# Up products of two feed-forward layers as seven block products in place of eight, and down products in five groups

## The chip, the cores and the metric

The kernel runs on one core of a Trainium2 chip. The metric is the device time of one execution in microseconds (us). TensorE (PE) does the matrix products, VectorE (DVE) and ScalarE (ACT) the elementwise work, GpSimd (POOL) some of it too, and SyncE (SP) issues most of the loads.

## The reference

Two layers act on 640 token columns (128 of a prompt, 512 of a sample) of width 1024. The first layer's mixer is a gated delta rule, the second's a neighbourhood attention. After each comes the part that the change touches:

```python
def conv_ffn(h, w_up, conv_w, conv_b, w_down):
    u = dwconv_centred(h @ w_up, conv_w) + conv_b
    val, gate = jnp.split(u, 2, axis=-1)
    return (jax.nn.silu(gate) * val) @ w_down
...
xs = xs + g2s * conv_ffn(rmsnorm(xs, norm2_g[l]) * (1.0 + sc2s) + sh2s,
                         ffn_w_up[l], ffn_conv_w[l], ffn_conv_b[l], ffn_w_down[l])
```

`w_up` is 1024 x 5632 (22 value tiles and 22 gate tiles of 128), `w_down` 2816 x 1024, and the convolution has three taps along the tokens, within the prompt and within the sample apart. Everything is float32.

## The kernel before

Activations lie with their features on the partitions and the 640 columns along the free side. A float32 product is made of three matmuls on a rounded part and a residue: every weight tile `w` is cast by ScalarE to `wh` (L376) and VectorE forms `wl = w - wh` (L378); h is kept as `hh` and `hl`, eight tiles of 128 features each. `pass3` then adds `wh*hh`, `wh*hl` and `wl*hh` in PSUM (L388, L389, L390), in two column halves of 384 and 256 (`HALVES_U`, `HALVES_R`).

`ffn` (one call per layer) goes over 22 pairs, value tile i (`uv`) and gate tile i (`ug`). For a pair `dense` loads each tile (512 KB), splits it and makes 8 x 2 x 3 matmuls into a PSUM tile `duv` or `dug`. Then `conv` scales with the middle tap on ScalarE (L440) and adds the outer taps on VectorE (L445; four instructions a tile, 511 and 127 columns), ScalarE takes silu of the gate, VectorE multiplies (L560), and the product is split again into `F` (L562, L563). After the groups of tiles 0 to 7 and 8 to 14, `into_residual` multiplies the group's F with the down weights (`wdn`) and adds the result to the residual X with `residual` (L454); the last group, 15 to 21, goes through `into_residual_split`, which does one column half after the other so that the next normalization (`hl` L348, `nt` L343) can start on the first.

The order on each engine is set by a scheduler from the written order, priorities and the pools' buffers; `chain` holds TensorE to the written order of products in the first layer. Weights pass through a ring of two tiles each of `wst`, `wh` and `wl`. `between` interleaves modulation sums (`ada_rows`: VectorE instructions of 512 columns, L252, on weights `adr` that the GpSimd queue loads) and, in the first layer, the preparation of attention bias tables. The first pair of a layer is made while the second half of h is still being normalized (`hooks`).

Of the kernel before, what the change touches and what calls it, by code (L numbers as in the profile page):

```python
# [57 lines left out]
GROUPS = ((0, 8), (8, 15), (15, 22))  # L58
# [29 lines left out]
class Net:  # L88
    def __init__(self, ctx, tc, a):
# [5 lines left out]
        self.wide = False  # L95
        self.hooks, self.strict = [], False
# [313 lines left out]
    def dense(self, src, name, base=UBASE, halves=HALVES_U):  # L410
        w = self.weights(src, KT, name)
        ps = self.pd.tile([128, 1024], F32, tag="d", name=f"d{name}")
        for cols in halves:
            self.prod(ps, base, w, KT, self.hmov, cols)
        return ps
# [4 lines left out]
    def dense_many(self, srcs, names, norm):  # L420
# [11 lines left out]
        return [ps for _, ps in out]  # L432

# [24 lines left out]

    def into_residual(self, srcs, kt, movs, l, gi, name, first={}, between=None):
        late = []  # L460
        for m in range(KT):
            w = first.get(m) or self.weights(srcs[m], kt, f"{name}{m}")
            ps = self.pd.tile([128, 1024], F32, tag="d", name=f"r{name}{m}")
            if m < 2:
                late.append((w, ps))
                for half in (0, 1):
                    self.prod(ps, RBASE, w, kt, movs, HALVES_R[half], ks=range(kt - 1))
                if m < 1:
                    continue
            else:  # L470
                late = [(w, ps)]
            for i, (w, ps) in enumerate(late, m + 1 - len(late)):
                for half in (0, 1):
                    self.prod(ps, RBASE, w, kt, movs, HALVES_R[half], ks=range(kt - 1, kt) if m < 2 else None)
                for half in (0, 1):
                    self.residual(ps, i, half, l, gi)
            if between and m > 1:
                between(None)

    def half_bank(self, name, i, half):  # L480
        if self.wide and i % 2 == 1:
            return self.pa.tile([128, 512], F32, tag="g", name=name)
        return self.pd.tile([128, 1024 if self.wide else 512], F32, tag="d", name=name)
# [41 lines left out]
    def ffn(self, l, fp, norm, norms, between=None):  # L525
# [3 lines left out]
        fcb = self.smv("fcb").rearrange("p (l t) -> p l t", l=2)[:, l]  # L529
        def hold(name, n):  # L530
            if name[-1] == "5":
                return fp.tile([128, 2 * W], F32R, tag="F", name=name, bufs=9)[:, 16 : 16 + n]
            size = KT if name[-1] in "01" else NFT - GROUPS[-1][0]
            return fp.tile([128, size * 128], F32R, tag=name[:2] + name[-1], name=name, bufs=1)[:, :n]

        for grp, (g0, g1) in enumerate(GROUPS):
            fs = []
            srcs = [a["w_dn"][l, m][:, g0 * 128 : g1 * 128] for m in range(KT)]
            first = {}
            for i in range(g0, g1):  # L540
                if i >= g1 - 2:
                    m = i - g1 + 2
                    first[m] = self.weights(srcs[m], g1 - g0, f"dn{l}{grp}{m}", None, hold)
                up, names = [a["w_up"][l, i], a["w_up"][l, NFT + i]], [f"uv{l}{i}", f"ug{l}{i}"]
                if i == 0:
                    with self.behind(self.marks):
                        pv, pg = self.dense_many(up, names, norm)
                else:
                    pv = self.dense(up[0], names[0])
                    if between:  # L550
                        between(None)
                    pg = self.dense(up[1], names[1])
                with self.tc.high_priority(FHP if i == g1 - 1 else 0):
                    yv = fp.tile([128, W], F32, tag="yv", name=f"yv{l}{i}", bufs=2)
                    yg = fp.tile([128, W], F32, tag="yg", name=f"yg{l}{i}", bufs=2)
                    self.conv(yv, pv, fcw[:, i], fcb[:, i : i + 1])
                    self.conv(yg, pg, fcw[:, NFT + i], fcb[:, NFT + i : NFT + i + 1])
                    c = slice(0, W)
                    nc.scalar.activation(yg[:, c], yg[:, c], AF.Silu)
                    nc.vector.tensor_tensor(yv[:, c], yv[:, c], yg[:, c], ALU.mult)  # L560
                    f = fp.tile([128, 2 * W], F32R, tag="F", name=f"F{l}{i}", bufs=9).rearrange("p (a w) -> p a w", a=2)
                    nc.scalar.copy(f[:, 0, c], yv[:, c])  # L562
                    nc.vector.tensor_tensor(f[:, 1, c], yv[:, c], f[:, 0, c].bitcast(F32), ALU.subtract)  # L563
                fs.append(f)
                if between:
                    between(i)
            movs = lambda k, fs=fs: (fs[k][:, 0, :], fs[k][:, 1, :])
            if g1 < NFT:
                self.into_residual(srcs, g1 - g0, movs, l, 5, f"dn{l}{grp}", first, between)
            else:  # L570
# [1094 lines left out]
```

## Time and profile before

| | |
|---|---|
| median of 3 runs | 1871.53 us (1865.12 to 1872.86) |
| the profiled execution | 1872.86 us, span 1871.1 us, granted TensorE clock 0.98 |
| first up product of the first layer, last of the second | 583.3 us, 1804.3 us |
| up products | 4224 matmuls (half of 384, half of 256 columns) |
| down products | 2112 matmuls, the same shapes |
| instructions of POOL in the whole span | 498 |

How to read the rows: in the table by stretches, `us, PE busy (x) PEld busy (x) DVE busy (x) ACT busy (x) POOL busy (x), PEclk, DMA share, GB/s` stand behind the window. In groups of instructions the columns are line, engine, operation, written tile <- read tiles, shapes and count | busy us, mean ns of one | idle time before them and its releasers. In the timeline they are start in us, duration in us, engine, line, operation, tiles, shape and count; in brackets the idle time before and who ended it.

### The profile page before, as it was taken

What the parts mean: (1) busy time and instruction counts of PE and PEld (TensorE: products, weight loads), DVE (VectorE), ACT (ScalarE), POOL (GpSimd) and SP (SyncE); (2) the same over time, 40 slices, a digit from 0 to 9 for tenths busy, and PEclk for the clock granted to TensorE, in tenths of its full rate; (3) what the DMA queues carried; (4) which work ended last, traced back from release to release, by engine and by line L of the source; (5) the groups of instructions that cost most, each with busy time, mean ns of one, the idle gap of its engine ahead of it and who ended that gap; (6) DMA issues with size and microseconds to landing.
All of it is one profiled execution on the core that took longest, in us unless ns stands there. A gap on an engine that the chain in (4) does not pass through costs nothing.

```text
span 1871.1 us, 34463 instructions
## 1 busy us (share of the span) xinstructions
PE 1790.4 (96%) x13587; PEld 1702.7 (91%) x13587; DVE 1257.4 (67%) x3093; ACT 725.9 (39%) x1461; POOL 290.3 (16%) x498
## 2 busy tenths in 40 slices
PE   6889999799999999999999999999999999999998
PEld 5878988598899999999999988888899999999998
DVE  6797867487678999754465799555689643543664
ACT  4553445264444341241243444444454322332343
POOL 0245103417003112100000212111141000000000
PEclk9898999799999999999999999999999999999999
DMA  7133233232242455441222344222334312222231
GB/s 299 61 85 108 54 124 108 76 96 61 64 158 86 155 182 163 132 163 54 87 90 80 124 152 139 75 78 65 96 107 136 102 48 78 88 62 77 89 92 57
DMA packets 102482, 194.17 MB, mean 104 GB/s; under 512 B 39496, under 2 KB 59034, under 8 KB 99560
## 3 DMA queue, kind: packets, MB, share of 16 engines
q1 hardware_dynamic: 93376, 161.57, 27.5%
q0 software_dynamic: 8400, 29.87, 5.2%
q8 instruction: 107, 1.75, 0.4%
q14 instruction: 55, 0.45, 0.1%
q10 hardware_dynamic: 544, 0.52, 0.1%
HBM read 183.09 MB, written 12.46 MB: 105 GB/s over the span
## 4 chain that ended last, share of the span: by engine, by line
PE 50%; DVE 4%; issue 2%; DMA 1%; ACT 1%; POOL 0%; DVEq 0%; POOLq 0%; ACTq 0%
PE duv L388 4%; PE duv L390 4%; PE duv L389 4%; PE dug L388 4%; PE dug L389 4%; PE dug L390 4%; PE rdn L388 4%; PE rdn L389 4%; PE rdn L390 4%; PE dqn L388 1%; PE dvn L388 1%; PE no L1346 1%; PE s L1289 1%; PE dvn L390 1%; PE dvn L389 1%
## 5 line engine op out<-in xcount | busy, mean ns | idle before, releaser
L388 PE MATMUL duv<-hh,whuv 128*128 128x256 f32 (+1 forms) x704 | 217.2, 309 | 5.9 <-DVE yv L445 4.0
L388 PE MATMUL rdn<-F,whdn 128*128 128x384 f32 (+1 forms) x704 | 216.1, 307 | 3.3 <-DVE X L454 3.3
L390 PE MATMUL duv<-hh,wluv 128*128 128x256 f32 (+1 forms) x704 | 216.7, 308 | 0.3 <-DVE wluv L378 0.3
L389 PE MATMUL duv<-hl,whuv 128*128 128x256 f32 (+1 forms) x704 | 216.5, 308 | 0.0
L389 PE MATMUL dug<-hl,whug 128*128 128x256 f32 (+1 forms) x704 | 215.9, 307 | 0.0
L390 PE MATMUL dug<-hh,wlug 128*128 128x256 f32 (+1 forms) x704 | 215.9, 307 | 0.0
L388 PE MATMUL dug<-hh,whug 128*128 128x256 f32 (+1 forms) x704 | 215.9, 307 | 0.0
L389 PE MATMUL rdn<-F,whdn 128*128 128x384 f32 (+1 forms) x704 | 215.5, 306 | 0.0
L390 PE MATMUL rdn<-F,wldn 128*128 128x384 f32 (+1 forms) x704 | 215.5, 306 | 0.0
L388 PEld LDWEIGHTS duv<-hh,whuv 128*128 128x128 f32 x704 | 132.8, 189 | 6.4 <-ACT yg L440 4.6
L388 PEld LDWEIGHTS rdn<-F,whdn 128*128 128x128 f32 x704 | 132.4, 188 | 4.0 <-issue 2.1
L454 DVE SCALAR_TENSOR_TENSOR X<-rdn,mods,X 128x128 f32<-128x128 f32 (+1 forms) x144 | 54.9, 434 | 117.6 <-PE rdn L390 117.4
L390 PEld LDWEIGHTS duv<-hh,wluv 128*128 128x128 f32 x704 | 132.9, 189 | 0.6 <-DVE wluv L378 0.6
L389 PEld LDWEIGHTS duv<-hl,whuv 128*128 128x128 f32 x704 | 132.7, 189 | 0.0
L388 PEld LDWEIGHTS dug<-hh,whug 128*128 128x128 f32 x704 | 132.4, 188 | 0.0
L390 PEld LDWEIGHTS dug<-hh,wlug 128*128 128x128 f32 x704 | 132.3, 188 | 0.0
L389 PEld LDWEIGHTS rdn<-F,whdn 128*128 128x128 f32 x704 | 132.2, 188 | 0.0
L390 PEld LDWEIGHTS rdn<-F,wldn 128*128 128x128 f32 x704 | 132.2, 188 | 0.0
L389 PEld LDWEIGHTS dug<-hl,whug 128*128 128x128 f32 x704 | 132.1, 188 | 0.0
L376 ACT CAST whdn<-wstdn 128x896 fp32r<-128x896 f32 (+1 forms) x48 | 47.0, 979 | 209.1 <-PE rdn L389 120.9
L376 ACT CAST whug<-wstug 128x1024 fp32r<-128x1024 f32 x44 | 46.2, 1050 | 142.9 <-PE dug L389 119.4
L378 DVE TENSOR_TENSOR wldn<-wstdn,whdn 128x896 fp32r<-128x896 f32 (+1 forms) x48 | 54.4, 1133 | 56.7 <-ACT whdn L376 56.7
(710 smaller groups left out, 4803.3 us busy)
## 6 DMA issues: line engine op xcount, KB each, us to landing
wstuv<-w_up SPq DMA_DIRECT2D x44, 512.0 KB, 3.5
wstug<-w_up SPq DMA_DIRECT2D x44, 512.0 KB, 3.6
adat<-w_ada SPq DMA_DIRECT2D x20, 1024.0 KB, 5.0
adr<-w_adar POOLq DMA_DIRECT2D x80, 256.0 KB, 3.2
wstdn<-w_dn SPq DMA_DIRECT2D x32, 448.0 KB, 3.4
wstdn<-w_dn SPq DMA_DIRECT2D x16, 512.0 KB, 3.6
adr<-w_adar SPq DMA_DIRECT2D x32, 256.0 KB, 2.9
wstqT<-w_gin SPq DMA_DIRECT2D x8, 512.0 KB, 4.4
```

The lines of the kernel that those rows point to most:

```text
L376: nc.scalar.copy(wh[:, c], st[:, c])
L378: ins = eng.tensor_tensor(wl[:, c], st[:, c], wh[:, c].bitcast(F32), ALU.subtract).ins
L388: nc.tensor.matmul(out, a, mh, start=first, stop=False)
L389: nc.tensor.matmul(out, a, ml, start=False, stop=False)
L390: ins = nc.tensor.matmul(out, b, mh, start=False, stop=last).ins
L454: nc.vector.scalar_tensor_tensor(x, ps[:, base + c0 : base + c1], self.mod(l, gi, m, v), x, ALU.mult, ALU.add)
L1289: nc.tensor.matmul(ss[e][:, o], qb[H[e]], kk[H[e]], start=True, stop=True, tile_position=(64 * e, 0))
L1346: nc.tensor.matmul(O[H[e], cb * 128 : cb * 128 + 128], v_, p_, start=(j == 0), stop=(j == 2), tile_position=(0, 64 * e),)
```

## The change

A pair's value and gate tiles, on the two halves of the 1024 features, form a 2 x 2 block matrix; h, on feature halves and column halves of 320, forms another. The product of 2 x 2 blocks is made with seven block products and sums of blocks (Winograd's form) rather than eight. Of each layer's 22 pairs the first two (`DIRECT`) stay ordinary products; while they run, `blocks` forms the sums of the moving side (`T0`, `T1`, `T2`, and, in place of the right half of the first four feature tiles, a fourth block). For the other 20 pairs `pair` forms sums of weight blocks on GpSimd (`s1`, `s2`, `g0`; L621, L624, L625, L628), casts seven quarters of 512 columns (L551, L552), makes seven products of 12 matmuls with 320 columns and combines them: ScalarE copies two to SBUF (`p1`, `p5`), VectorE makes five adds that read PSUM (L630, L633, L635, L637, L640), GpSimd adds two (L631, L638). The convolution then reads `cv` and `cg` in SBUF, not PSUM. Of the first layer's seven residues, those of products 1 and 3 are formed by GpSimd (`POOLED`).

The downs go in groups of tiles 0-3, 4-7, 8-11, 12-15 and 16-21; a group's downs follow the ups of the pair after it. Eight of the layer-1 modulation vectors' tiles (m = 2) are summed during the attention and not in the first feed-forward layer; the interleaving of the other sums changes. TensorE is held to the written order in the second layer too.

```diff
-GROUPS = ((0, 8), (8, 15), (15, 22))
+GROUPS = ((0, 4), (4, 8), (8, 12), (12, 16), (16, 22))
+NH = W // 2
+DIRECT = 2
+POOLED = ((1, 3), ())
...
+    def quarter(self, src, name, lo=None):
...
+        nc.scalar.copy(wh, src)
+        (lo or nc.vector).tensor_tensor(wl, src, wh.bitcast(F32), ALU.subtract)
...
+    def blocks(self):
+        nc, TT = self.nc, self.nc.vector.tensor_tensor
+        lo, hi = slice(0, NH), slice(NH, W)
+        for k in range(4):
+            b = self.B[k]
+            for i in range(2):
+                nc.gpsimd.tensor_tensor(
+                    b[:, i], self.hh[:, k + 4 * i].bitcast(F32), self.hl[:, k + 4 * i].bitcast(F32), ALU.add
+                )
+            b11, b12, b21, b22 = b[:, 0, lo], b[:, 0, hi], b[:, 1, lo], b[:, 1, hi]
+            TT(b11, b12, b11, ALU.subtract)
+            TT(b12, b22, b12, ALU.subtract)
+            TT(b22, b22, b11, ALU.subtract)
+            TT(b21, b21, b22, ALU.subtract)
+            for t, x in zip(self.T, (b11, b22, b12)):
+                nc.scalar.copy(t[:, k, 0], x)
+                TT(t[:, k, 1], x, t[:, k, 0].bitcast(F32), ALU.subtract)
...
+    def pair(self, l, i, fp, pf):
...
+        P, V = nc.gpsimd.tensor_tensor, nc.vector.tensor_tensor
...
+        P(s1, g0, g1, ALU.add)
+        x = product(5, s1, self.tmov(0), L)
+        nc.scalar.copy(p5, x)
+        P(s2, s1, v0, ALU.subtract)
+        P(g0, v0, g0, ALU.subtract)
+        x = product(1, v0, first, L)
+        nc.scalar.copy(p1, x)
+        P(s1, v1, s2, ALU.subtract)
+        x = product(6, s2, self.tmov(1), L)
+        V(cg1, x, p1, ALU.add)
+        P(cv1, cg1, p5, ALU.add)
+        x = product(3, s1, last, R)
+        V(cv1, x, cv1, ALU.add)
+        x = product(2, v1, last, L)
+        V(cv0, x, p1, ALU.add)
+        x = product(7, g0, self.tmov(2), L)
+        V(cg0, x, cg1, ALU.add)
+        P(cg1, cg0, p5, ALU.add)
+        x = product(4, g1, first, R)
+        V(cg0, x, cg0, ALU.add)
...
-        sums = net.ada_rows([(1, m, t) for m in (3, 4) for t in range(KT)], self.ap_, 2, self.nc.sync)
+        sums = net.ada_rows([(1, m, t) for m in (2, 3, 4) for t in range(KT)], self.ap_, 2, self.nc.sync)
```

The order of instructions shows the change in three places. In these rows the names are written tile <- read tiles with the buffer's number. First VectorE in the second layer, where two pairs follow one another with no downs between. Before (`wluv`, `wlug` residues, L445 taps):

```order
L378 TENSOR_TENSOR wluv_18946<-wstuv_18943,whuv_18945 128x1024
L445 SCALAR_TENSOR_TENSOR yv_18926<-duv_18822,sm,yv_18926 128x127
L445 SCALAR_TENSOR_TENSOR yv_18926<-duv_18822,sm,yv_18926 128x511
L445 SCALAR_TENSOR_TENSOR yv_18926<-duv_18822,sm,yv_18926 128x127
L445 SCALAR_TENSOR_TENSOR yv_18926<-duv_18822,sm,yv_18926 128x511
L378 TENSOR_TENSOR wlug_19001<-wstug_18998,whug_19000 128x1024
L445 SCALAR_TENSOR_TENSOR yg_18927<-dug_18877,sm,yg_18927 128x127
L445 SCALAR_TENSOR_TENSOR yg_18927<-dug_18877,sm,yg_18927 128x511
L445 SCALAR_TENSOR_TENSOR yg_18927<-dug_18877,sm,yg_18927 128x127
L445 SCALAR_TENSOR_TENSOR yg_18927<-dug_18877,sm,yg_18927 128x511
L560 TENSOR_TENSOR yv_18926<-yv_18926,yg_18927 128x640
L563 TENSOR_TENSOR F_18940<-yv_18926,F_18940 128x640
```

Now, of the 23 rows of such an interval, those in its middle (`wlp` are residues of quarters, `pp` the products in PSUM, `s_19043` the next pair's sum from GpSimd):

```order
L552 TENSOR_TENSOR wlp_18954<-s_18892,whp_18953 128x512
L552 TENSOR_TENSOR wlp_18954<-wsv_18890,whp_18953 128x512
L694 TENSOR_TENSOR yv_18871<-yv_18871,yg_18872 128x640
L630 TENSOR_TENSOR cg_18897<-pp_18938,p_18894 128x320
L552 TENSOR_TENSOR wlp_18988<-wsg_18888,whp_18987 128x512
L697 TENSOR_TENSOR F_18885<-yv_18871,F_18885 128x640
L633 TENSOR_TENSOR cv_18896<-pp_18957,cv_18896 128x320
L552 TENSOR_TENSOR wlp_18988<-wsg_18888,whp_18987 128x512
L635 TENSOR_TENSOR cv_18896<-pp_18973,p_18894 128x320
L552 TENSOR_TENSOR wlp_19051<-s_19043,whp_19050 128x512
L552 TENSOR_TENSOR wlp_19051<-wsv_19041,whp_19050 128x512
L637 TENSOR_TENSOR cg_18897<-pp_18991,cg_18897 128x320
```

Adds from PSUM now stand between the residues, and the residue of product 4 (the second `wlp_18988`) stands behind the add L633.

Second, GpSimd in the second layer. Before, the loads of `adr` end its work until the last normalization:

```order
L234 DMA adr_16648<-w_adar 128x512
L234 DMA adr_16654<-w_adar 128x512
L308 TENSOR_TENSOR nstf_19875<-nstf_19875,mhalf 128x3
L308 TENSOR_TENSOR nstf_20095<-nstf_20095,mhalf 128x2
L1661 UNCONDITIONAL_BRANCH
```

Now six instructions stand there for each of 20 pairs (of one pair's interval, between two L638):

```order
L638 TENSOR_TENSOR cg_18593<-cg_18593,p_18591 128x320
L621 TENSOR_TENSOR s_18892<-wsg_18888 128x512
L624 TENSOR_TENSOR s_18893<-s_18892,wsv_18890 128x512
L625 TENSOR_TENSOR wsg_18888<-wsv_18890,wsg_18888 128x512
L631 TENSOR_TENSOR cv_18743<-cg_18744,p_18742 128x320
L628 TENSOR_TENSOR s_18892<-wsv_18890,s_18893 128x512
L638 TENSOR_TENSOR cg_18744<-cg_18744,p_18742 128x320
```

The add L631, for which VectorE's L633 waits, stands behind the three sums of the next pair.

Third, VectorE at the end of the second layer's two direct pairs (`B` are the moving side's blocks, `duv_16754` the second pair's product, `s_16917` the first sum of pair 2). Before there is no such work: taps and residues follow as in the first fence. Now:

```order
L592 TENSOR_TENSOR hl<-B_16521,hh 128x320
L459 SCALAR_TENSOR_TENSOR yv_16868<-duv_16754,sm,yv_16868 128x256
L459 SCALAR_TENSOR_TENSOR yv_16868<-duv_16754,sm,yv_16868 128x127
L459 SCALAR_TENSOR_TENSOR yv_16868<-duv_16754,sm,yv_16868 128x255
L459 SCALAR_TENSOR_TENSOR yv_16868<-duv_16755,sm,yv_16868 128x255
L459 SCALAR_TENSOR_TENSOR yg_16869<-dug_16762,sm,yg_16869 128x127
L459 SCALAR_TENSOR_TENSOR yv_16868<-duv_16755,sm,yv_16868 128x256
L459 SCALAR_TENSOR_TENSOR yg_16869<-dug_16762,sm,yg_16869 128x256
L459 SCALAR_TENSOR_TENSOR yg_16869<-dug_16762,sm,yg_16869 128x127
L459 SCALAR_TENSOR_TENSOR yg_16869<-dug_16762,sm,yg_16869 128x255
L459 SCALAR_TENSOR_TENSOR yg_16869<-dug_16763,sm,yg_16869 128x255
L552 TENSOR_TENSOR wlp_16925<-s_16917,whp_16924 128x512
```

The first residue of pair 2 (`wlp_16925`) stands behind the blocks and ten taps of pair 1; L592, the last of four such rows, writes over a right half of `hl` that the second direct pair reads to its end.

More of the change, by code (lines that the diff above doesn't have):

```diff
@@ L456, in residual @@
                 )
[L459 to L478, printed above, removed]
     def half_bank(self, name, i, half):
+        if self.banks:
+            self.turn += 1
+            pool, tag, bufs = self.banks[self.turn % len(self.banks)]
+            return pool.tile([128, 512], F32, tag=tag, name=name, bufs=bufs)
         if self.wide and i % 2 == 1:
@@ new lines, in downs @@
+    def downs(self, l, grp, fs):
+        g0, g1 = GROUPS[grp]
+        n = g1 - g0
+        for m in range(KT):
+            st = self.wp.tile([128, KT * 128], F32, tag="wst", name=f"wsd{l}{grp}{m}", bufs=WSTB)
+            self.load = self.nc.sync.dma_start(st[:, : n * 128], self.a["w_dn"][l, m][:, g0 * 128 : g1 * 128]).ins
+            w = self.quarter(st[:, : n * 128], f"dn{l}{grp}{m}")
+            for half, c in enumerate(HALVES_R):
+                ps = self.half_bank(f"rdn{l}{grp}{m}{half}", 0, half)
+                self.prod(ps, -c[0], w, n, lambda k: (fs[g0 + k][:, 0], fs[g0 + k][:, 1]), c)
+                with self.tc.high_priority(HP):
+                    self.residual(ps, m, half, l, 5, -c[0])
@@ L526, in ffn @@
+    def ffn(self, l, fp, pf, norm, norms, between=None):
         nc, a = self.nc, self.a
@@ L529, in ffn @@
         fcb = self.smv("fcb").rearrange("p (l t) -> p l t", l=2)[:, l]
+        last = len(GROUPS) - 1
         def hold(name, n):
[L531 to L569, printed above, removed]
-            else:
-                return self.into_residual_split(
-                    srcs, g1 - g0, movs, l, 5, f"dn{l}{grp}", norms, hold, (6, 7), first=first
-                )
@@ L1378, in run @@
                     next(dense, None)
-                if i > 1:
-                    next(sums, None)
+                next(sums, None)
             for _ in dense:
```

159 lines of the change are left out of this document (135 added, 24 removed).

## The prediction

> **What bounds the kernel now.** I read the busy shares of the page first, then the busy time by stretches, then the feed-forward products one by one, and last the places where VectorE and GpSimd work at the same time.
>
> ```profile
> PE 1790.4 (96%) x13587; PEld 1702.7 (91%) x13587; DVE 1257.4 (67%) x3093; ACT 725.9 (39%) x1461; POOL 290.3 (16%) x498
> ...
> 650.00:700.00 50.00, 50.00 (x349) 50.00 (x348) 49.61 (x103) 20.83 (x25) 8.20 (x15) 1.00 0.56 172
> ...
> 1600.00:1650.00 50.00, 50.00 (x344) 50.00 (x344) 30.38 (x46) 20.60 (x24) 0.00 (x0) 1.00 0.31 98
> ```
>
> In both feed-forward layers (the second row is from the first, the third from the second) TensorE has no gap. VectorE is full in the first layer, where the modulation sums lie, and 61% busy in the second; GpSimd has next to nothing. TensorE is the limit, and its price is the distance of two starts, not the recorded duration, since matmuls overlap:
>
> ```profile
> 902.25 0.28 PE L388 MATMUL rdn<-F,whdn 128*128 128x256 f32 x1
> 902.37 0.28 PE L389 MATMUL rdn<-F,whdn 128*128 128x256 f32 x1
> ...
> 902.76 0.34 PE L389 MATMUL duv<-hl,whuv 128*128 128x384 f32 x1
> 902.94 0.34 PE L390 MATMUL duv<-hh,wluv 128*128 128x384 f32 x1
> ```
>
> Starts lie 0.114 us apart at 256 columns (three in 0.34) and 0.173 at 384, so a 320-column product takes about 0.1435. A pair of up tiles is 96 matmuls averaging 320 columns, 13.8 us. A group of downs over four tiles, 8 x 24 matmuls, is 27.55 us.
>
> **The matmuls.** A pair now has 7 x 12 = 84 matmuls of 320 columns, 12.05 us: 1.72 us less, 69 us over the 40 pairs so made. That is the whole gain, and it needs the other engines to keep up with 12.05 us. Their prices:
>
> ```profile
> L445 DVE SCALAR_TENSOR_TENSOR yg<-dug,sm,yg 128x511 f32<-128x511 f32 x88 | 65.1, 740 | 0.0
> L445 DVE SCALAR_TENSOR_TENSOR yg<-dug,sm,yg 128x127 f32<-128x127 f32 x88 | 30.1, 342 | 1.8 <-ACT yg L440 1.7
> 966.83 1.91 DVE L445 SCALAR_TENSOR_TENSOR yv<-duv,sm,yv 128x127 f32<-128x127 f32 x4
> L378 DVE TENSOR_TENSOR wlne<-wstne,whne 128x512 fp32r<-128x512 f32 x8 | 5.5, 683 | 0.7 <-ACT whne L376 0.7
> L560 DVE TENSOR_TENSOR yv<-yv,yg 128x640 f32<-128x640 f32 x44 | 36.2, 823 | 25.1 <-ACT yg L559 25.1
> L708 DVE TENSOR_TENSOR dec<-gb,ngc 128x512 f32<-128x512 f32 x16 | 10.9, 678 | 2.6 <-PE gb L702 2.5
> L708 DVE TENSOR_TENSOR dec<-gb,ngc 128x256 f32<-128x256 f32 x8 | 3.3, 411 | 0.7 <-PE gb L702 0.7
> L252 DVE CUSTOM_DVE_ANT_0 adj<-adr,cb,sm 128x512 f32<-128x512 f32 x56 | 41.7, 745 | 6.0 <-DMA adr<-w_adar 6.0
> L454 DVE SCALAR_TENSOR_TENSOR X<-rdn,mods,X 128x256 f32<-128x256 f32 x96 | 43.0, 476 | 4.9 <-PE rdn L390 4.9
> L376 ACT CAST whne<-wstne 128x512 fp32r<-128x512 f32 x8 | 4.9, 618 | 4.2 <-PE dvn L389 2.0 <-PE rne L389 1.5 <-ACT Ps L1220 0.3
> ...
> 1352.92 1.29 POOL L378 TENSOR_TENSOR wlno<-stg,whno 128x512 fp32r<-128x512 f32 x1 [22.87 <-ACT whno L376]
> L1199 POOL TENSOR_TENSOR bias<-bias,mask 128x248 f32<-128x248 f32 x32 | 19.7, 636 | 41.8 <-DMA bias<-cols 41.6
> ```
>
> On VectorE the four taps of a convolution, 740 + 740 + 342 + 342 = 2.16, took 1.91 back to back, so each instruction costs its duration less about 0.08. A pair of the second layer then asks of VectorE:
> - seven weight residues of 512, 7 x 0.61 = 4.3;
> - eight taps, 4 x 0.66 + 4 x 0.26 = 3.7;
> - the gate product and F's residue, 2 x 0.75 = 1.5;
> - five new adds that read PSUM, 320 columns, between the two `dec` rows: 0.48 - 0.08 = 0.4 each, 2.0.
>
> Together 11.5 us. ScalarE: seven casts at 0.62 and some 4 us for two copies, two taps, silu and F, 8.4 us. GpSimd: four sums of 512 at 1.29 and two adds of 320 at about 0.85 (between 0.64 and 1.29), 6.9 us. Each alone would fit under 12.05.
>
> **VectorE and GpSimd exclude each other.** This row of evidence decides the case:
>
> ```profile
> 48.81 3.02 DVE L343 SCALAR_TENSOR_TENSOR nt<-X,scg,rsb 128x256 f32<-128x256 f32 x2
> 49.07 2.47 POOL L378 TENSOR_TENSOR wlkT<-wstkT,whkT 128x1024 fp32r<-128x1024 f32 x1 [20.31 <-ACT whkT L376]
> ...
> 313.75 1.23 DVE L378 TENSOR_TENSOR wlqT<-wstqT,whqT 128x1024 fp32r<-128x1024 f32 x1 [0.28 <-ACT whqT L376]
> 313.86 1.46 POOL L826 TENSOR_TENSOR lP<-lN,lY 80x156 f32<-80x156 f32 x1
> 315.41 0.49 POOL L832 TENSOR_TENSOR lY<-lY,lP 80x156 f32<-80x156 f32 x1
> ...
> 316.33 0.69 DVE L911 TENSOR_TENSOR dec<-kq3s,dec 128x512 f32<-128x512 f32 x1
> 316.58 0.53 POOL L832 TENSOR_TENSOR lY<-lY,lP 80x175 f32<-80x175 f32 x1
> ```
>
> Two `nt` instructions, both inputs in SBUF, took 3.02 us: the second, issued while GpSimd ran, ended at 51.8, 0.3 after GpSimd's 2.47 us. The other way round GpSimd's `lP` took 1.46 instead of about 0.49, because it waited for `wlqT`. Where VectorE has one input in PSUM (`dec<-kq3s`), neither is slowed. In a pair 4.3 + 3.7 + 1.5 = 9.5 us of VectorE are now of the excluding kind (the taps too: they read `cv` and `cg` in SBUF, and read PSUM before), and GpSimd's 6.9 us are. They add: 9.5 + 6.9 = 16.4 us, more than 12.05 and more than the 13.8 before. If the PSUM adds also find no cover it is 18.4. Adds and waits alternate between the two engines (VectorE's second `cv` add waits for GpSimd's, which stands behind three sums), so I take 17.0, nearer the lower end because in the rows above an engine starts as soon as the other ends.
>
> The Trainium skill ("SBUF — State Buffer", section "A bandwidth-pool intuition that's wrong (but worth ruling out)") gives, for descriptors that GpSimd writes, about 115 ns from VectorE's end to the blocked work's end; as an estimate for each of six to eight GpSimd instructions in twenty pairs it would add 16 us to the sum. The trace disagrees: `lP` less its own 0.49 began at 314.83, no later than the end of `wlqT` at 314.98. I add nothing.
>
> **The sum.** I divide a layer into 19 intervals, from one pair's last add to the next's, and take from the order of the rows which instructions each holds. Before, they cost 19 x 13.8 + 4 x 27.55 = 372 us a layer.
> - Second layer: ten full intervals at 17.0; four with only 3.0 us of GpSimd work, 9.5 + 3.0, taken as 13.0 (12.05 to 15); one with twelve sum instructions, 18.0 + 4.4 = 22.3; four with a down group at 40.5 (TensorE alone 39.6, exclusive work 26). 170 + 52 + 22 + 162 = 406, so +34.
> - First layer: two residues move to GpSimd (-1.2 there, +2.6 here) and sums are added: ten full at 18.2 by addition, taken as 19.1; two of about 22.8 with many sums; three light at 14.6; four with downs, 43.1, 43.5 and twice 40.5. 191 + 46 + 44 + 168 = 448, so +76.
> - Pair 2 is shorter too: -3.4 for both layers.
> - Start of a layer. The blocks of the moving side are eight GpSimd adds of 640 columns (1.6 each, between the 512 and 1024 prices) and 28 VectorE instructions of 320 (0.41): 24 us, exclusive. They need h complete, which by the rows below is 12 us after the first up product, and TensorE has 27.6 us of direct pairs: 15.6 us remain for 24 plus the second pair's own residues. Behind them stand, after the direct products end, three residues and ten taps, 1.2 + 3.6 us, and pair 2's first residue, 0.6: 5.4 us that nothing covers. Between 5.4 and 20 a layer I take 12: +24.
> - Sixteen modulation sums move into the attention: 32 x 0.75 = 24 us of VectorE. It is 95% busy in the first heads (row below), with TensorE 48 of 50. Between 0 and 24 I take +4; later heads have room.
> - Two more groups of downs: 96 further residual instructions, some 34 us of VectorE, read PSUM and lie under the down products (13 us of VectorE in 27.55): nothing. The last group has six tiles and its matmuls are only redistributed: nothing. Weight loads move the same bytes at a DMA share of 0.31: nothing.
>
> ```profile
> L388 PE MATMUL duv<-hh,whuv x704: 276/306/525, 583.3 to 1804.3; 128*128 128x384 f32 x88, 128*128 128x256 f32 x88
> 594.48 0.87 DVE L348 SCALAR_TENSOR_TENSOR hl<-nt,mods,hh 128x256 fp32r<-128x256 f32 x2
> 1090.00:1140.00 50.00, 48.02 (x371) 41.77 (x371) 47.48 (x139) 21.23 (x52) 9.81 (x18) 1.00 0.50 155
> ```
>
> 34 + 76 - 3 + 24 + 4 = 135. The profiled execution took 1872.9 (span 1871.1), 1.3 above the median of 1871.5: 1872.9 + 135 = 2008 us. With every wait hidden and only the additions left (full intervals 16.4 and 18.2, start 5.4, attention 0) it is 1968; with 18.4 and 20.6 in the full intervals, light ones at 15 and 17, 20 at each start and 24 in the attention, 2093.
>
> **Rivals.**
> - *Faster: GpSimd's sums fall beside VectorE's PSUM adds and idle time, and do not exclude.* An interval is then the larger of 12.05 and VectorE's own 11.5, with the sums 12.3 to 14.2 in the first layer: 22 us less in the second layer, 5 in the first, 3 at pair 2, 11 more at the starts, 1853 us. It decides once 2.6 of the 6.9 us a pair (16.4 - 13.8) lie beside other work. For it: VectorE has 2.0 us of PSUM adds a pair. Against it: that is less than 2.6, and the overlaps above.
> - *Exclusive work moves into the downs.* In a group of four pairs of the second layer it is 70 us, TensorE 76. If buffers let it spread, that layer costs 345 (-27), the first its 407 (+35), the starts +24: about 1902. Against it: the weight ring holds four quarters, 7 us of products, so little can be prepared ahead.
> - *The change does not cut the matmuls.* The order has 480 TensorE rows fewer, 40 x 12: excluded.
>
> **Chances.** The addition, 1968 to 2093: 0.62; worse: 0.05; spread into the downs: 0.16; no exclusion: 0.15; else 0.02. The range 1885 to 2095 leaves out the faster rival and the worst. About 0.5% is what a measurement can tell from no change; so faster 0.15, same 0.05, slower 0.80.
>
> **What would show it.** In the profile after, up products with 320 columns start 0.144 apart but wait for VectorE's residues and ScalarE's casts; an interval between downs lasts 16 to 19 us; GpSimd's sums of 512 last well over 1.29 us, or VectorE's residues over 0.68; a stall stands at pair 2 of each layer; downs stay gapless. I am wrong if GpSimd keeps 1.29 beside unslowed residues, or if TensorE stays without gaps in the ups.

## The result and the profile after

The changed kernel took 2063.23 us (median; 2059.61 to 2066.61), the kernel before beside it 1872.19: ratio 1.1027, 95% interval 1.0992 to 1.1063. The forecast was 2008 (1885 to 2095), so slower as forecast, by 191 us where 135 were worked out. The profiled execution has a span of 2063.1 us, against 1871.1 before: 192.0.

First the busy shares of the page, and the chain of work that ended last:

```profile
PE 1797.1 (87%) x13107; PEld 1685.5 (82%) x13107; DVE 1670.6 (81%) x3661; ACT 851.7 (41%) x1813; POOL 695.5 (34%) x778
...
PE 39%; DVE 35%; issue 10%; POOL 6%; DMA 6%; ACT 3%; SPq 1%; DVEq 0%; POOLq 0%; ACTq 0%
```

TensorE has 480 matmuls fewer (13107, 13587 before), but fell from 96% to 87% of the span, and VectorE carries a third of the chain. What TensorE waited for stands in the table of waits (us in total, times, longest):

```profile
PE pp L395 <- DVE wlp L552: 129.0, 65, 13.7
...
PE pp L395 <- POOL wlp L552: 28.0, 14, 6.2
```

These are the weight residues, on VectorE and, in the first layer, on GpSimd. Next, groups of instructions by form (line, engine, operation, tiles, shapes and count | busy us, mean ns of one):

```profile
L459 DVE SCALAR_TENSOR_TENSOR yv<-cv,sm,yv 128x511 f32<-128x511 f32 x80 | 89.7, 1121 | 0.0
L552 DVE TENSOR_TENSOR wlp<-wsg,whp 128x512 fp32r<-128x512 f32 x80 | 70.4, 890 | 0.2 <-ACT whp L551 0.2
L697 DVE TENSOR_TENSOR F<-yv,F 128x640 fp32r<-128x640 f32 x44 | 57.1, 1297 | 1.4 <-ACT F L696 1.4
L640 DVE TENSOR_TENSOR cg<-pp,cg 128x320 f32<-128x320 f32 x40 | 19.1, 479 | 2.1 <-POOL cg L638 2.1
...
L625 POOL TENSOR_TENSOR wsg<-wsv,wsg 128x512 f32<-128x512 f32 x40 | 63.7, 1592 | 0.0
L621 POOL TENSOR_TENSOR s<-wsg 128x512 f32<-128x512 f32 x40 | 61.5, 1537 | 94.3 <-DVE wlp L552 84.4 <-issue 8.5
```

VectorE instructions with two SBUF inputs are stretched: taps of 511 columns to 1121 ns (740 before, from PSUM), residues of 512 to 890 (683), F's residue to 1297 (824). Those that read PSUM are not (L640, 479 ns for 320 columns, as priced). GpSimd's four sums rose from 1.29 us to between 1.47 and 1.59. So "busy" on both engines now contains waiting.

The intervals between one pair's last add and the next's, from tiles 6 to 9 of the second layer (the same columns as in the tables by stretches before):

```profile
1687.10:1703.40 16.30, 13.38 (x79) 12.85 (x78) 15.44 (x23) 7.05 (x12) 7.55 (x6) 0.90 0.21 64
1703.40:1720.50 17.10, 14.52 (x86) 14.26 (x87) 15.10 (x24) 8.41 (x14) 9.12 (x6) 0.90 0.16 47
1720.50:1734.20 13.70, 13.31 (x90) 12.88 (x89) 12.84 (x22) 6.75 (x12) 3.40 (x3) 1.00 0.24 78
1734.20:1774.10 39.90, 39.90 (x280) 39.90 (x279) 31.84 (x57) 13.68 (x23) 12.68 (x9) 1.00 0.27 86
```

Two full intervals of 16.3 and 17.1 us, a light one of 13.7, and one with a group of downs, 39.9, in which TensorE has no gap. From pair 6 on that is the pattern of the second layer; the first three intervals, with the last modulation sums in them, took 16.2, 23.2 and 46.7 us.

Where the 192.0 us lie, from the places of the first and last matmuls and last adds in both traces (a stage's own length after less that before; before, one tile's downs, 6.9 us, are counted with the intervals and not with the end, as the last group now has six tiles; the last up product of before, that of gate tile 21, ends at 1811.7 us, and the 1804.3 of the table further up is the last of value tile 21):

| stage | first layer | second layer | forecast |
|---|---|---|---|
| start: first up product to pair 2's last add (before: to its last matmul) | 78.8 - 45.1 = +33.7 | 76.8 - 47.3 = +29.5 | +10.3 each (12 - 1.7) |
| 19 intervals to pair 21's last add | 475.9 - 377.6 = +98.3 | 412.1 - 377.9 = +34.2 | +76, +34 |
| end of the layer | 38.8 - 42.6 = -3.8 | 40.1 - 42.6 = -2.5 | 0 |
| attention between the layers | 350.2 - 344.8 = +5.4 | | +4 |
| up to the first layer | -2.8 | | 0 |

### The profile page after: what moved, and what is told of

The parts are those of the page before. It is cut to its first block, busy times and chain, and to the rows that moved or that the text cites. A ratio compares the mean times of both kernels' runs of the same rounds, so it can differ in the third digit from the quotient of the medians.

```text
span 2063.1 us, 35116 instructions
## 1 busy us (share of the span) xinstructions
PE 1797.1 (87%) x13107; PEld 1685.5 (82%) x13107; DVE 1670.6 (81%) x3661; ACT 851.7 (41%) x1813; POOL 695.5 (34%) x778
## 4 chain that ended last, share of the span: by engine, by line
PE 39%; DVE 35%; issue 10%; POOL 6%; DMA 6%; ACT 3%; SPq 1%; DVEq 0%; POOLq 0%; ACTq 0%
DVE yv L459 5%; DVE wlp L552 5%; DVE yg L459 4%; DVE adj L257 3%; DVE adr L257 2%; PE rdn L395 2%; PE rdn L394 2%; PE rdn L393 2%; PE pp L395 2%; PE pp L394 2%; PE pp L393 2%; DVE F L697 1%; PE p L999 1%; DVE X L484 1%; DVE wldn L552 1%
## 5 line engine op out<-in xcount | busy, mean ns | idle before, releaser
L395 PE MATMUL pp<-hh,wlp 128*128 128x320 f32 x640 | 214.4, 335 | 80.3 <-DVE wlp L552 52.0
L395 PE MATMUL pp<-T,wlp 128*128 128x320 f32 x448 | 150.8, 337 | 77.2 <-DVE wlp L552 77.0
L393 PE MATMUL pp<-hh,whp 128*128 128x320 f32 x640 | 207.8, 325 | 4.0 <-ACT whp L551 4.0
L394 PE MATMUL pp<-hl,whp 128*128 128x320 f32 x640 | 207.1, 324 | 0.0
L395 PEld LDWEIGHTS pp<-hh,wlp 128*128 128x128 f32 x640 | 129.1, 202 | 95.4 <-DVE wlp L552 62.8
L393 PE MATMUL pp<-T,whp 128*128 128x320 f32 x448 | 147.0, 328 | 21.8 <-ACT whp L551 21.8
L393 PE MATMUL rdn<-F,whdn 128*128 128x384 f32 (+1 forms) x496 | 153.4, 309 | 0.0
L394 PE MATMUL rdn<-F,whdn 128*128 128x384 f32 (+1 forms) x496 | 153.3, 309 | 0.0
L394 PE MATMUL pp<-T,whp 128*128 128x320 f32 x448 | 146.2, 326 | 0.0
L459 DVE SCALAR_TENSOR_TENSOR yv<-cv,sm,yv 128x127 f32<-128x127 f32 (+1 forms) x160 | 134.0, 892 | 8.4 <-ACT yv L453 8.4
L393 PEld LDWEIGHTS pp<-hh,whp 128*128 128x128 f32 x640 | 129.8, 203 | 4.5 <-ACT whp L551 4.5
L394 PEld LDWEIGHTS pp<-hl,whp 128*128 128x128 f32 x640 | 129.1, 202 | 0.0
L551 ACT CAST whp<-s 128x512 fp32r<-128x512 f32 x112 | 68.5, 617 | 104.3 <-PE pp L394 63.5
L624 POOL TENSOR_TENSOR s<-s,wsv 128x512 f32<-128x512 f32 x40 | 60.5, 1513 | 115.1 <-DMA wsv<-w_up 105.8
```

The costliest lines, as they stand in the source:

```text
L393: nc.tensor.matmul(out, a, mh, start=first, stop=False)
L394: nc.tensor.matmul(out, a, ml, start=False, stop=False)
L395: ins = nc.tensor.matmul(out, b, mh, start=False, stop=last).ins
L459: nc.vector.scalar_tensor_tensor(y[:, a:b], t[:, a + sh - lo : b + sh - lo], wv[:, tap : tap + 1], y[:, a:b], ALU.mult, ALU.add,)
L551: nc.scalar.copy(wh, src)
L624: P(s2, s1, v0, ALU.subtract)
```

## Experiments

Every run was timed beside the kernel before; ratios are to that kernel. Line numbers of a variant differ by a few from the changed kernel's.

### The sums on VectorE

```diff
-POOLED = ((1, 3), ())
+POOLED = ((), ())
...
-        P, V = nc.gpsimd.tensor_tensor, nc.vector.tensor_tensor
+        P, V = nc.vector.tensor_tensor, nc.vector.tensor_tensor
```

> The four sums and two adds of every pair, and the first layer's two residues on GpSimd, move to VectorE; the blocks' adds at a layer's start stay on GpSimd. Theory (VectorE's SBUF instructions and GpSimd's exclude each other): a pair of the second layer asks of both engines together 9.3 + 6.9 = 16.2 us now, and 11.4 + 4 x 0.61 + 2 x 0.41 = 14.7 on VectorE alone, so the full intervals fall from 16.2-17.2 us to 14.7-15.0, and that layer by 10 to 45 us; in the first layer GpSimd's second half intervals of 16 to 20 us fall to about 15. Together 1995 us (1960 to 2020). Rival (no exclusion; VectorE, 81% busy, is the limit by its own count of instructions): 150 us of added VectorE work make it slower than the changed kernel, 2110 or more.

Measured: 1992.52 us, ratio 1.0651 (1.0629 to 1.0673). The busy shares:

```profile
PE 1774.0 (89%) x13107; PEld 1672.2 (84%) x13107; DVE 1633.8 (82%) x3941; ACT 856.4 (43%) x1813; POOL 308.8 (16%) x498
```

VectorE does 280 instructions more, and its busy time is 37 us shorter: the waiting that it no longer does is worth more than the work that it took over. The same four intervals of the second layer (the windows show which share of each VectorE fills):

```profile
1625.80:1637.60 11.80, 11.61 (x80) 11.35 (x78) 11.77 (x25) 6.62 (x12) 0.00 (x0) 1.00 0.26 90
1637.60:1655.80 18.20, 14.57 (x87) 14.00 (x88) 17.27 (x34) 8.49 (x14) 0.00 (x0) 0.91 0.13 44
1655.80:1669.20 13.40, 12.62 (x86) 12.35 (x85) 13.15 (x28) 7.41 (x13) 0.00 (x0) 1.00 0.27 79
1669.20:1709.50 40.30, 40.30 (x282) 40.30 (x281) 31.32 (x65) 13.68 (x23) 0.00 (x0) 1.00 0.28 86
```

The three without downs average 14.5 us, the 14.7 of the addition, unevenly shared out. All waits between sums, products and adds are still there, though a sum now takes 0.69 us in place of about 1.5, and every residue of 512 takes 0.69 as it did undisturbed. That points to the two engines holding each other up, and not to the waits as such. The time of the whole came out as the theory said; the layers took 531.3 and 514.0 us (593.5 and 529.0 in the changed kernel). The first layer's residues moved as well; moving them alone took 25 of its 62 us off (see below).

### No sums

```diff
-        P(s1, g0, g1, ALU.add)
-        x = product(5, s1, self.tmov(0), L)
+        x = product(5, g1, self.tmov(0), L)
...
-        x = product(6, s2, self.tmov(1), L)
+        x = product(6, v0, self.tmov(1), L)
         V(cg1, x, p1, ALU.add)
-        P(cv1, cg1, p5, ALU.add)
-        x = product(3, s1, last, R)
-        V(cv1, x, cv1, ALU.add)
+        x = product(3, v1, last, R)
+        V(cv1, x, p5, ALU.add)
```

> Leaves out the weight sums and the two adds on GpSimd: the seven products are made on raw quarters, so another thing is computed with the same casts, residues, matmuls and PSUM adds. Theory (exclusion): in the second layer GpSimd has nothing left in a pair, VectorE's 11.4 us fit under TensorE's 12.45 (start to start of a product 1.78 us), full intervals fall from 16.2-17.2 to 12.5-13 us, the layer's intervals from 412 to about 350; the first layer, with VectorE's modulation sums left, loses 60 to 80; together 1915 us (1890 to 1945). Rival (GpSimd's work lies beside VectorE's and costs nothing by itself): within 20 us of 2063.

Measured: 1899.7 us, ratio 1.0147 (1.0123 to 1.0170). The intervals of the second layer, again three and one with downs:

```profile
1563.90:1576.20 12.30, 12.30 (x86) 12.30 (x85) 11.02 (x23) 7.21 (x13) 0.00 (x0) 1.00 0.23 85
1576.20:1588.60 12.40, 12.40 (x87) 12.40 (x86) 12.30 (x25) 8.29 (x15) 0.00 (x0) 1.00 0.19 65
1588.60:1600.90 12.30, 12.30 (x84) 12.30 (x84) 11.02 (x22) 7.01 (x13) 0.00 (x0) 1.00 0.27 88
1600.90:1641.50 40.60, 40.60 (x280) 40.60 (x279) 27.21 (x56) 13.17 (x24) 0.00 (x0) 1.00 0.26 85
```

Here TensorE is the limit, at 12.3 us a pair, and no gap is left. VectorE's instructions in an interval are nearly those of the changed kernel (23, 25 and 22; 23, 24 and 22); only GpSimd's are gone, and 16.3, 17.1 and 13.7 became 12.3, 12.4 and 12.3. The four together fell from 87.0 to 77.6 us. And yet this kernel is 1.5% slower than the one before: its second layer took 468.1 us, no less than the 467.8 before, since the start keeps what the intervals gain.

### No block products

```diff
-            if i < DIRECT:
+            if i < DIRECT[l]:
...
-DIRECT = 2
+DIRECT = 22, 22
```

> All 22 pairs of each layer as ordinary products, five groups of downs, 16 modulation sums in the attention as in the changed kernel: the change without its block products. Theory (the loss is in the block products alone, the downs' groups cost nothing, the attention 5.4 us): 1880 us (1870 to 1890). Rival (more groups, with 96 further residual instructions on VectorE and more weight switches, cost time in the first layer): 1900 or more.

Measured: 1859.33 us, ratio 0.9944 (0.9927 to 0.9962). Both expectations missed: the rest of the change does not cost 8 us, it gains about 10, and this version is 0.6% faster than the kernel before. The first layer took 462.7 us (465.3 before), the attention 350.9 (344.8), the second layer 458.0 (467.8). So the groups of downs and their 96 further residual instructions are free, as the prediction took them, and the loss of 191 us lies in the block products. (Every second ordinary pair also takes one PSUM bank from another pool, here and in the other runs that change `DIRECT`.) Part of the gain of the second layer can be seen in stretches of ordinary up products, the first two of the kernel before, the third of this one (the number behind PE's busy time is the count of matmuls):

```profile
1430.00:1510.00 80.00, 80.00 (x547) 80.00 (x546) 56.81 (x102) 30.96 (x36) 2.69 (x5) 1.00 0.35 109
1720.00:1810.00 90.00, 90.00 (x631) 90.00 (x630) 53.63 (x81) 36.34 (x43) 0.00 (x0) 1.00 0.32 97
```

```profile
1495.00:1545.00 50.00, 50.00 (x349) 50.00 (x348) 26.35 (x50) 18.65 (x27) 0.00 (x0) 1.00 0.20 64
```

TensorE is gapless in all three, with a granted clock of 1.00, and still a matmul takes 0.146 us in the first, 0.143 in the others. Over the 270 us in which the second layer before kept the slower pace this is some 6 us. What brings the slower pace, and whether the change takes it away or it comes and goes, stays open.

### The blocks on VectorE

```diff
-                nc.gpsimd.tensor_tensor(
+                nc.vector.tensor_tensor(
                     b[:, i], self.hh[:, k + 4 * i].bitcast(F32), self.hl[:, k + 4 * i].bitcast(F32), ALU.add
                 )
```

> The eight adds that form the moving side's blocks at a layer's start go to VectorE (6 us) from GpSimd (12.1 us back to back, in which one VectorE instruction took 12.8 us). Theory (the start is late because GpSimd's adds stand behind the weights of pair 2 and the loads of the modulation weights on its queue, and then lock VectorE out): first product of pair 2 earlier by 6 to 15 us a layer, together 2040 us (2025 to 2055). Rival (the start is only as long as VectorE's own work): 6 us more a layer, 2075.

Measured: 2043.69 us, ratio 1.0927 (1.0910 to 1.0943). First come rows from the start of the second layer in the changed kernel, in the timelines of VectorE, GpSimd and TensorE (start, duration, engine, line, operation, tiles, shape, count, and in brackets the idle time before and who ended it):

```profile
1535.42 0.88 DVE L353 SCALAR_TENSOR_TENSOR hl<-nt,mods,hh 128x256 fp32r<-128x256 f32 x2
...
1549.02 12.84 DVE L257 CUSTOM_DVE_ANT_0 adj<-adr,cb,sm 128x512 f32<-128x512 f32 x1
...
1562.59 0.49 DVE L579 TENSOR_TENSOR B<-B 128x320 f32<-128x320 f32 x1
...
1574.99 1.29 DVE L592 TENSOR_TENSOR hl<-B,hh 128x320 fp32r<-128x320 f32 x3
1576.20 1.51 DVE L459 SCALAR_TENSOR_TENSOR yv<-duv,sm,yv 128x256 f32<-128x256 f32 x4
...
1579.71 0.69 DVE L552 TENSOR_TENSOR wlp<-s,whp 128x512 fp32r<-128x512 f32 x1
```

```profile
1542.84 1.29 POOL L624 TENSOR_TENSOR s<-s,wsv 128x512 f32<-128x512 f32 x1 [4.22 <-DMA wsv<-w_up]
1544.09 2.26 POOL L625 TENSOR_TENSOR wsg<-wsv,wsg 128x512 f32<-128x512 f32 x1
...
1548.68 0.54 POOL L239 DMA_DIRECT2D adr<-w_adar  x1 [0.56 <-DVE mods L257]
1549.24 12.08 POOL L575 TENSOR_TENSOR B<-hh,hl 128x640 f32<-128x640 f32 x8
```

```profile
1554.74 0.28 PE L395 MATMUL dug<-hh,wlug 128*128 128x256 f32 x1
1566.14 0.63 PE L393 MATMUL pp<-T,whp 128*128 128x320 f32 x1 [11.12 <-ACT whp L551]
1566.57 0.47 PE L394 MATMUL pp<-T,whp 128*128 128x320 f32 x1
1580.45 0.63 PE L395 MATMUL pp<-T,wlp 128*128 128x320 f32 x1 [13.41 <-DVE wlp L552]
```

The last of h is ready at 1536.3, 12.1 us after the first up product at 1524.2. The blocks' eight adds begin only at 1549.2. GpSimd works in order, and ahead of them stand pair 2's sums, which wait for its weights, and loads of modulation weights, which wait for VectorE's sums. Then the eight adds run back to back for 12.1 us, and one VectorE instruction of 0.75 us takes 12.84: it waits for all eight. VectorE forms the blocks from 1562.6 to 1576.3, then ten taps of the pair before, then pair 2's first residue at 1579.7. The ordinary products ended at 1555.0, and TensorE stands until 1580.4 but for two matmuls.

With the adds on VectorE the first product of pair 2 begins at the end of the ordinary products, yet the residue still stands behind the same run:

```profile
1541.45 0.31 PE L394 MATMUL pp<-T,whp 128*128 128x320 f32 x1
1561.16 0.64 PE L395 MATMUL pp<-T,wlp 128*128 128x320 f32 x1 [19.40 <-DVE wlp L552]
```

The blocks themselves begin no earlier in the second layer: 25.7 us after the first up product (25.0 in the changed kernel; 23.9 against 26.1 in the first layer); on VectorE taps, gate product and modulation sums stand ahead of them. Nor were pair 2's sums what held them up most: in the two runs that have no such sums on GpSimd ("The sums on VectorE", "No sums") the adds began 21.2 to 24.0 us after the first up product. The starts fell from 78.8 and 76.8 to 72.1 and 70.1 us. The gain of 6 to 15 us a layer was at its lower end, 6.7, though the first product itself came 11 us earlier in relation to the end of the ordinary ones. (The layers as a whole are 5.4 us shorter each; the rest of the 20 us lies in stages that the edit does not touch, see below.)

### Three ordinary pairs

```diff
-DIRECT = 2
+DIRECT = 3, 3
...
-            if i == 0:
+            if i == 0 and DIRECT[l] < NFT:
                 self.blocks()
```

> Three ordinary pairs at each layer's start, and the blocks formed after the second, so that 41 us of ordinary products lie over them in place of 28. Theory (the start is an uncovered run of VectorE and GpSimd work: blocks, their residues, ten taps, the first residue): 13.8 us more cover, less 4 us for the third pair's own residues and taps, so the excess of a start falls from 29 to 34 us to 17 to 24, plus 1.35 for the eighth product: 2043 us (2028 to 2055). Rival (the stall follows the blocks wherever they stand): 2063 to 2068.

In the kernel that ran, the blocks are still formed after the first pair, as the edit shows, and not after the second as the expectation has it: their adds begin 22.8 and 24.4 us after the first up product. Measured: 2040.08 us, ratio 1.0930 (1.0902 to 1.0959). From the first up product to pair 4's last matmul the layers take 106.4 and 105.3 us in place of 117.9 and 113.3; as a whole 579.4 and 523.1 in place of 593.5 and 529.0. The time came out near the theory's 2043, but by luck: most of the stall is still there, in the third ordinary pair:

```profile
1541.44 0.69 PE L393 MATMUL duv<-hh,whuv 128*128 128x384 f32 x1 [7.33 <-ACT whuv L381]
1556.54 0.69 PE L395 MATMUL duv<-hh,wluv 128*128 128x384 f32 x1 [14.08 <-DVE wluv L383]
```

These two waits, 21.4 us, stand in place of 11.12 and 13.41 (in the first layer 8.79 and 12.11 in place of 10.64 and 13.71): the third pair's own residue stands behind the blocks on VectorE. The pair that stalls, pair 2 in both kernels, takes 37.7 and 37.9 us in place of 42.7 and 41.6, and pair 4 gains more, 16.5 and 17.7 in place of 25.2 and 22.8. So the run does not show that a longer cover hides the blocks. (The run on the second layer alone, below, does form them after the second of three pairs.)

### The first layer's residues back on VectorE

```diff
-POOLED = ((1, 3), ())
+POOLED = ((), ())
```

> One edit on the changed kernel: the first layer's residues of products 1 and 3 go back from GpSimd to VectorE. Theory (exclusive work adds up, and GpSimd's queue is in order): 2 x (1.29 - 0.61) = 1.4 us less a pair, 27 us in 20 pairs, and TensorE's waits for residues behind GpSimd's adds go too; the second half of the first layer (pair 12's add to pair 21's, 230.7 us now) should take what the second layer takes there, 205.6. Together 2028 us (2010 to 2040). Rival (VectorE's own count of instructions is the limit of the first layer): 24 us more on VectorE, 2087.

Measured: 2026.55 us, ratio 1.0849 (1.0825 to 1.0872). The first layer fell from 593.5 to 568.1, as much as expected, but not at the place expected: the stretch of 230.7 us (it begins at pair 11's add, not at pair 12's as the expectation has it) is 228.8 now, while the nine intervals ahead of it fell from 245.2 to 222.6. The steady pattern of the second layer appears in the first only from pair 17 on (16.3 and 17.1 us); pairs 13 and 14 took 20.4 and 26.3. Why this is so stays open.

### Short modulation sums

```diff
+                x = n if queue is nc.sync else 64
                 nc.vector.tensor_tensor_reduce(
-                    junk, w, self.cb[:, v, h * n : h * n + n], 1.0, init, ALU.mult, ALU.add, out
+                    junk[:, :x], w[:, :x], self.cb[:, v, h * n : h * n + x], 1.0, init, ALU.mult, ALU.add, out
                 )
```

> The changed kernel with the modulation sums of both feed-forward layers taken over 64 of each 512 columns (another thing is computed; the loads, their order and every other instruction stay). Each of 96 VectorE instructions in the first layer and 32 in the second falls from 0.67 to about 0.15 us, 50 and 17 us. Theory (in the stretches with sums VectorE and GpSimd work one after the other without room, so what is taken away comes off the time): first layer shorter by 35 to 50, second by 10 to 17, together 2008 us (1995 to 2020). Rival (the sums fill idle time of VectorE, and the first layer is long because of GpSimd's residues): 2050 or more.

Measured: 2018.66 us, ratio 1.0811 (1.0777 to 1.0845). The second layer is 12.8 us shorter (expected 10 to 17), the first 25.3, less than the 35 expected at least. So the sums are not free beside GpSimd's work, which before they were in a first layer without a gap on TensorE; but half of the 50 us taken away did not come off the time. TensorE still waits 111 us for VectorE's residues and 26 us for GpSimd's, in place of 129 and 28.

### The second layer alone, and the modulation sums back

```diff
+DIRECT = 22, 3
...
+            if i == 1 and DIRECT[l] < NFT:
                 self.blocks()
...
+        P, V = nc.vector.tensor_tensor, nc.vector.tensor_tensor
...
+                nc.vector.tensor_tensor(
                     b[:, i], self.hh[:, k + 4 * i].bitcast(F32), self.hl[:, k + 4 * i].bitcast(F32), ALU.add
```

> Block products in the second layer alone, in the form that the earlier runs favour: sums, adds and blocks on VectorE, three ordinary pairs ahead; the first layer as ordinary products. Theory (without GpSimd, VectorE's 14.7 us a pair is the limit between the downs, and the downs' room isn't used): second layer about 489 us against 458 with ordinary products, together 1893 us (1875 to 1905). Rival (TensorE is the limit once nothing excludes, 12.3 us a pair): 1845.

Measured: 1896.94 us, ratio 1.0154 (1.0129 to 1.0178); second layer 494.4 us against 458.0 with ordinary products. Without GpSimd the block products still lose 36 us in the layer where VectorE had the most room. The start shows what forming the blocks later gives: they begin 36.5 us after the first up product, 7 us before the ordinary products end, and TensorE still waits 17.9 us for pair 3's first residue.

```diff
-        sums = net.ada_rows([(1, m, t) for m in (2, 3, 4) for t in range(KT)], self.ap_, 2, self.nc.sync)
+        sums = net.ada_rows([(1, m, t) for m in (3, 4) for t in range(KT)], self.ap_, 2, self.nc.sync)
```

The first layer sums m = 2 again, three of its sums a pair from the sixth pair on in place of two.

> The kernel without block products (1859.3), with the sixteen modulation sums moved back from the attention into the first feed-forward layer. Theory (they cost the attention some 4 to 6 us and are hidden in the first layer, whose VectorE is busy 342 of 463 us): attention 345 in place of 351 us, 1855 us (1848 to 1862). Rival (the attention has room for them): 1859 to 1862.

Measured: 1860.45 us, ratio 0.9954 (0.9939 to 0.9968): no different from 1859.33. The attention took 348.5 us against 350.9. The rival holds: the moved sums cost the attention nothing that can be told.

## Why the prediction was right, and where it was off

**TensorE's price.** Right. A pair of block products takes 12.3 us where nothing hinders it (12.05 was worked out: starts are 0.147 apart in the rows, not 0.1435), which leaves a saving of 1.5 us a pair, not 1.72. Six of the eight groups of downs between the pairs ran without a gap, in 27.7 to 28.4 us; the first of each layer waited, 0.7 us in the first layer and 3.9 in the second, where it took 34.7. The saving in the pairs was there to be had, and was not had, because TensorE was not the limit of the full intervals.

**Exclusion, and its sum.** Right, and the size nearly: the second layer's intervals came to 412 us against 406, full ones 16.2 to 17.2 against 17.0, light ones 13.8 to 14.5 against 13.0, those with downs 39.9 to 46.7 against 40.5. That the difference to before came out as +34.2 against +34 is luck, as before they took 378 us where 372 were worked out. The two runs on it tell it from its rivals. Taking GpSimd's work away brought the intervals down to TensorE's limit; giving the same work to VectorE, with every dependency kept, made the kernel 71 us faster while VectorE had 280 instructions more. The rival without exclusion needed 2.6 us of GpSimd's 6.9 beside other work; 16.3 and 17.1 us a pair lie above the 13.8 from which it decides. Its price of 1853 was too low: with the pairs' sums and adds left out altogether the time is 1900, with the starts still long.

The Trainium skill ("SBUF — State Buffer", section "SBUF: two separate sides") calls the port that the two engines share an exclusive lock, held for a whole instruction by the one that starts first. The trace agrees that the two exclude each other. It does not bear out that the one that starts first gets it: by its record VectorE's instruction of 12.84 us began 0.22 us ahead of GpSimd's eight adds, and it ended after the last of them.

**Spread into the downs.** Wrong, as held. VectorE is busy 31.8 of the 39.9 us of an interval with downs while the next interval is limited by it; the same with the sums on VectorE (31.3 of 40.3).

**Start of a layer.** The step that failed. "They need h complete, ... 12 us after the first up product, and TensorE has 27.6 us of direct pairs: 15.6 us remain" took the blocks to begin when their input is ready. They began 25 us after the first up product, behind GpSimd's own queue, with 6 us of cover left. Which work ahead of them set that time is shown in part only: in all runs with two ordinary pairs they began 21 to 26 us after it, without pair 2's sums ahead of them and on VectorE too, which points to the first pair's work on VectorE as well. The 24 us of exclusive work and the 5.4 us tail behind it were right in size (1549.2 to 1580.4 is 31 us) but stood almost whole on the path. The starts cost 33.7 and 29.5 us, 12 and at most 20 had been taken, and this is 42.6 of the missing 57. The adds on VectorE took 11 us off the two layers, a third ordinary pair 20. Neither takes the stall away, as VectorE's run of blocks, taps and residue, some 24 us, stays: with three pairs it holds up the third, and where the blocks were formed a pair later it followed them (17.9 us).

**First layer's intervals.** Second in size: 475.9 against 448. The step is the price of the four intervals with downs, 43.1, 43.5 and twice 40.5, which came to 52.3, 55.8, 48.5 and 43.7; the fifteen others took 275.6 against 280. In the first two lie eleven modulation sums of two instructions each:

```profile
701.40:753.70 52.30, 43.72 (x283) 42.28 (x281) 50.64 (x98) 13.79 (x23) 24.68 (x25) 0.97 0.38 122
808.10:863.90 55.80, 44.53 (x293) 43.22 (x291) 53.88 (x99) 13.29 (x22) 26.80 (x28) 0.96 0.38 120
```

VectorE is busy for 97% of them. The third, 48.5 us, holds no such sums: there TensorE waited 2.41 and 4.52 us for GpSimd's residues. By the prices of undisturbed instructions (1.04 ns a column and 0.08 us, as the rows of before give it) VectorE's work in SBUF in each of the first two is 28.7 us, its work from PSUM 9.4 and GpSimd's 17.0: 55.1 in all, against 52.3 and 55.8. So of the 9.4 us from PSUM at most 3 found cover, where I had counted them as covered by the downs. In the second layer about half of their 2.1 us a pair did (17.4 us of all three against 16.3 in one interval, 18.6 against 17.1 in the next). The residues on GpSimd (25 us by the run that moved them back) and the sums (25 us) both carry it; the two runs cannot be added up, and the share of each stays open.

**Attention, more groups, weight loads.** +5.4 us against 4, but the run with the sums moved back shows no cost, and the stage took 347 to 351 us in all but one of the variants (357 with the sums on VectorE), with the sums moved back too: the +4 cannot be told from nothing. Stages that an edit does not touch differ by some microseconds from kernel to kernel; the first up product came between 574 and 583 us. So the terms of the table are good to about 5 us. More groups cost nothing, as said; that the rest of the change would gain 10 us was not foreseen.

**What would show it.** Residues went well over 0.68, sums over 1.29 (1.47 to 1.59), and the stall stands at pair 2 of each layer: as listed. Downs are gapless but for the first group of each layer. The products wait for VectorE's residues (129 us) far more than for casts (26).

**The bounds.** The terms that the prediction names for its lower and upper bound add up to 1976 and 2088; for the last 8 and 5 us of 1968 and 2093 it shows no working. The result lies inside either way.

## What to carry to other kernels

Fewer matmuls pay only if the elementwise work that replaces them fits under the shorter time, and on VectorE and GpSimd it is to be added up, not compared, where VectorE's instructions take both inputs from SBUF as GpSimd's do. Before trusting that a preparation is covered, look at what stands ahead of it in the queue of the engine that does it: an input that is ready at 12 us does not help if the queue gets there at 25. More cover does not help either, if the covering work needs the same engine behind the preparation. When a change of several parts loses, run the parts: here the blocks lost 200 us and the rest gained 10.

## What the runs showed of the hardware

- GpSimd's run of eight adds without a break kept a 0.75 us VectorE instruction waiting for 12.84 us, and the other way round a GpSimd residue of 1.29 us took 7.61 while VectorE formed the first layer's blocks one instruction after another:

```profile
625.75 7.61 POOL L552 TENSOR_TENSOR wlp<-wsv,whp 128x512 fp32r<-128x512 f32 x1 [7.06 <-ACT whp L551]
```

  It ended at 633.36, so its own 1.29 us began at about 632.1, when VectorE had gone over to taps that read PSUM. But the two can also alternate: in the runs without sums and with three ordinary pairs the same eight adds took 14.4 us in the second layer, and VectorE's instructions of 0.48 us beside them 1.8 each. What decides between the two patterns stays open.

- A long wait cost TensorE twice. After the stall of 13.41 us in the second layer, matmuls of 320 columns start 0.267 us apart for 5.5 us, and only then 0.147:

```profile
1580.88 0.47 PE L393 MATMUL pp<-T,whp 128*128 128x320 f32 x1
1581.15 0.47 PE L394 MATMUL pp<-T,whp 128*128 128x320 f32 x1
...
1585.68 0.46 PE L393 MATMUL pp<-hh,whp 128*128 128x320 f32 x1
1585.95 0.34 PE L394 MATMUL pp<-hl,whp 128*128 128x320 f32 x1
```

The granted clock of the start is 0.81 (1524.2 to 1596.6 us), before 0.96 in the same stage. The Trainium skill ("TensorE: Matmul & The Clock Gate", section "Part 1: The HAM clock gate (the "warmup" mystery)") gives columns divided by 1.2 GHz as the distance after an idle stretch; 320 / 1.2 GHz is 0.267, and the trace agrees. The prediction had no term for it. In the block products of the changed kernel 410 starts lie 0.2 to 0.3 us apart, 47 us more than at 0.147; in the run without sums 141, 16 us more. How much of it is on the path no run separates.
